# The last three down units of a decoder block, split 384 + 128 tokens in place of 256 + 256

## The chip, the cores and the metric

The kernel runs on one core of a Trainium2 chip. The metric is device time in microseconds (us). TensorE (PE, with its weight loads shown apart as PEld) multiplies into PSUM, VectorE (DVE) and ScalarE (ACT) read PSUM and work element by element, GpSimd (POOL) does a little early on, and SyncE (SP) issues all the loads and stores. A number in brackets after a kernel's time is the lowest and highest of its runs.

## The reference

One decoder block on a sequence of 512 tokens and 1024 channels: a mixer, then a squared-ReLU MLP, then a final RMSNorm. Only the end bears on this case:

```python
for i in range(DEPTH):                       # DEPTH = 1
    ...
    h = rmsnorm(x, norm_mlp_w[i]) * (1.0 + scale_f) + shift_f
    x = x + gate_f * (jnp.square(jax.nn.relu(h @ w_up[i])) @ w_down[i])
return rmsnorm(x, norm_final_w)
```

`w_down` is 4096 x 1024. The final norm needs, for each token, the mean square over all 1024 channels, so no token can be scaled before its last channel block is there.

## The kernel before, in words

Channels lie on the 128 partitions and tokens along the free dimension, so the 1024 channels of x are eight tiles of 128 x 512 (`x1[j]`, held in two large `xs` buffers). Each weight is loaded as float32 and split by `load_unit` into a high and a low float32r part (`hl` buffers, lines 131 and 132); activations are split in the same way (`s` buffers). A product is made of three matmuls, high times high, high times low, low times high (`mm3`, lines 141 to 143), and a "unit" is 8 blocks of 128 input channels, so 24 matmuls into one PSUM bank (`ps`). Every matmul loads its 128 x 128 weights anew.

The MLP goes over the 4096 hidden channels in four quarters. In the last quarter the output blocks j = 0 to 4 are made as whole units over 512 tokens. The last three, j = 5, 6, 7, are computed in two stretches of tokens: their weights are loaded once, then for each stretch the three units are multiplied over its tokens alone (72 matmuls), and after each unit come, on those tokens:

- `residual` (line 663 on DVE, 667 or 670 on ACT, 671 on DVE): x gets the gated unit added, its squares go into the running sum `ssum`, or for the last unit into `last_sq`; then line 754 on ACT scales x by the norm's weight.
- `norm` after the third unit: `column_sums` turns the squares into one sum for each token with matmuls of one moving column, one per 128 tokens and tile of squares (line 167 opens the sums, line 170 adds `ssum`, then `last_sq`); `rstd` makes square root (line 176, ACT) and reciprocal (line 177, DVE), puts them on the diagonal of one 128 x 128 block per 128 tokens (even blocks on DVE, line 183; odd ones on ACT, line 181), and spreads them over all partitions with one matmul that is as wide as the stretch (line 185).
- four multiplications on DVE (line 759), two channel tiles each over the stretch, and behind each a store on SP's queue (line 760).

The matmuls of lines 167, 170 and 185 have plain float32 operands, and each is executed as two weight loads and two matmul records. Those of lines 141 to 143 are one record each.

The order on each engine in this part is set by a scheduler at build time: it may place the norm's matmuls of the first stretch between the second stretch's unit matmuls. Each engine then works its list strictly in order. The `HALVES` of line 658 are (0, 256) and (256, 512).

## Time and profile before

| what | value |
|---|---|
| time, median of 3 runs | 998.27 us (997.61 to 998.98) |
| profiled execution: time | 997.95 us |
| profiled execution: span of its instructions | 996.2 us |
| mean granted TensorE clock | 0.992 |
| TensorE busy | 973.7 us, 98% of the span |
| VectorE busy | 623.8 us, 63% |
| ScalarE busy | 482.3 us, 48% |
| first unit matmul of the split part | 967.83 us |
| last unit matmul of the split part starts | 986.50 us |

Times within the profile count from the span's start. The profiled execution's own time is 1.75 us above its span, and it lies 0.32 us under the median. A busy share counts overlapping records as busy; what is worth reading in the end part is the distance between the starts of neighbouring instructions. In the groups a line of `rstd` or `column_sums` may belong to the first norm, the second or the last one.

### The profile page before, as it was taken

Reading aid. Unit: us, or ns where it says so; the run is one execution under the profiler, and the core shown is the slowest. Engines: PE = TensorE matmul, PEld = TensorE weight load, DVE = VectorE, ACT = ScalarE, POOL = GpSimd, SP = SyncE. Lnnn points to the kernel's source line nnn. Section 1 sums busy time; section 2 is a strip of 40 time slices with the busy share of each in tenths; the row PEclk is TensorE's granted clock in tenths of the full one; section 3 lists DMA queues with packets and bytes.
Section 4 is the critical chain, followed back from the end, with each engine's and each line's share of the span. In section 5 each row is a group of like instructions: output and inputs, shape, how many; then the busy total and the mean of one; then the engine's idle time right before and its main releaser. Section 6 shows DMA issues by size and latency. Waiting matters only on the chain.

```text
span 996.2 us, 12196 instructions
## 1 busy us (share of the span) xinstructions
PE 973.7 (98%) x4732; PEld 802.8 (81%) x4732; DVE 623.8 (63%) x887; ACT 482.3 (48%) x718; POOL 84.7 (9%) x79
## 2 busy tenths in 40 slices
PE   7899999999999999999999999999999999999996
PEld 6678777888778878788888888988888888888886
DVE  5978877586777776979775565654344334434443
ACT  5277999579648932553422343443133223313342
POOL 3510210211012012210000000000000000000000
PEclk8999999999999999999999999999999999999998
DMA  9725542442354233436886444032323232232302
GB/s 355 278 92 172 152 124 91 125 136 88 90 134 125 88 114 95 127 106 220 279 272 200 137 167 162 1 111 101 101 89 106 85 106 89 102 106 85 106 1 85
DMA packets 58620, 129.55 MB, mean 130 GB/s; under 512 B 4609, under 2 KB 29313, under 8 KB 58562
## 3 DMA queue, kind: packets, MB, share of 16 engines
q1 hardware_dynamic: 58562, 128.77, 40.1%
q8 instruction: 37, 0.61, 0.3%
q14 instruction: 21, 0.17, 0.1%
HBM read 126.53 MB, written 2.23 MB: 129 GB/s over the span
## 4 chain that ended last, share of the span: by engine, by line
PE 79%; ACT 8%; DVE 7%; DMA 2%; issue 2%; POOL 1%; SPq 1%; DVEq 0%; ACTq 0%; POOLq 0%
PE ps L141 25%; PE ps L142 24%; PE ps L143 24%; DMA mt<-cs_d 2%; ACT hl L131 1%; ACT L433 1%; DVE sz L157 1%; DVE xs L157 1%; PE ps L470 1%; PE ps L454 1%; ACT L350 1%; PE ps L447 1%; PE ps L281 1%; ACT L378 1%; DVE s L271 1%
## 5 line engine op out<-in xcount | busy, mean ns | idle before, releaser
L141 PE MATMUL ps<-s,hl 128*128 128x512 f32 (+1 forms) x1272 | 490.9, 386 | 1.3 <-ACT pad L529 1.2
L142 PE MATMUL ps<-s,hl 128*128 128x512 f32 (+1 forms) x1272 | 486.4, 382 | 0.0
L143 PE MATMUL ps<-s,hl 128*128 128x512 f32 (+1 forms) x1272 | 486.4, 383 | 0.0
L131 ACT CAST hl<-raw 128x1024 fp32r<-128x1024 f32 (+1 forms) x161 | 167.4, 1042 | 276.4 <-PE ps L142 269.0
L141 PEld LDWEIGHTS ps<-s,hl 128*128 128x128 f32 x1272 | 239.3, 188 | 50.4 <-issue 3.5
L142 PEld LDWEIGHTS ps<-s,hl 128*128 128x128 f32 x1272 | 239.4, 188 | 46.8 <-issue 1.4
L143 PEld LDWEIGHTS ps<-s,hl 128*128 128x128 f32 x1272 | 239.3, 188 | 46.8 <-issue 1.0
L132 DVE TENSOR_TENSOR hl<-raw,hl 128x1024 fp32r<-128x1024 f32 x153 | 189.9, 1243 | 126.5 <-ACT hl L131 123.5
L663 DVE SCALAR_TENSOR_TENSOR xs<-ps,mod,xs 128x512 f32<-128x512 f32 (+1 forms) x46 | 31.3, 680 | 106.8 <-PE ps L143 106.7
L111 ACT CAST s<-sz 128x512 fp32r<-128x512 f32 x52 | 31.5, 620 | 52.9 <-DVE sz L709 42.3
L157 DVE CUSTOM_DVE_ANT_0 raw<-raw,cbc,par_t 128x1024 f32<-128x1024 f32 x32 | 40.9, 1279 | 19.1 <-DMA raw<-adaT 19.0
L112 DVE TENSOR_TENSOR s<-sz,s 128x512 fp32r<-128x512 f32 x52 | 35.0, 689 | 22.8 <-ACT s L111 22.7
L433 ACT ACTIVATE mt<-mt,ncs 128x128 f32<-128x128 f32 x128 | 41.7, 392 | 13.2 <-POOL mt L429 12.9
L346 DVE SCALAR_TENSOR_TENSOR s<-ps,par_t,s 128x511 f32<-128x511 f32 (+2 forms) x54 | 40.2, 744 | 7.4 <-ACT s L344 6.9
L281 PE MATMUL ps<-s,hl 128*128 128x512 f32 x144 | 36.7, 410 | 5.8 <-ACT s L266 5.8
L281 PEld LDWEIGHTS ps<-s,hl 128*128 128x128 f32 x144 | 27.5, 196 | 14.3 <-ACT s L266 7.9
L429 POOL TENSOR_SCALAR_AFFINE_SELECT mt<-mt 128x1024 f32<-128x1024 f32 x16 | 19.5, 1224 | 215.4 <-ACT cd L426 99.0
L350 ACT ACT_TABLE_LOAD x19 | 24.4, 1283 | 7.0 <-DVE s L346 6.7
L433 ACT ACT_TABLE_LOAD x20 | 25.7, 1283 | 0.3
L492 ACT ACTIVATE s<-sz 128x512 f32<-128x512 f32 x16 | 10.1, 628 | 26.6 <-DVE sz L491 26.6
L111 ACT CAST s<-s 128x512 fp32r<-128x512 f32 x16 | 9.9, 622 | 25.5 <-DVE s L542 25.3
L709 DVE TENSOR_TENSOR sz<-sz 128x512 f32<-128x512 f32 x32 | 21.7, 684 | 0.0
(164 smaller groups left out, 783.7 us busy)
## 6 DMA issues: line engine op xcount, KB each, us to landing
raw<-adaT SPq DMA_DIRECT2D x32, 512.0 KB, 4.2
raw<-wup SPq DMA_DIRECT2D x32, 512.0 KB, 3.3
raw<-wdn SPq DMA_DIRECT2D x32, 512.0 KB, 3.3
raw<-wx SPq DMA_DIRECT2D x18, 512.0 KB, 3.5
raw<-wz SPq DMA_DIRECT2D x16, 512.0 KB, 4.0
mt<-cs_d SPq DMA_DIRECT2D x16, 512.0 KB, 5.9
raw<-wbs SPq DMA_DIRECT2D x16, 512.0 KB, 3.3
raw<-wgate SPq DMA_DIRECT2D x16, 512.0 KB, 3.7
```

The source lines that it names most:

```text
L111: act.copy(hi, src)
L112: dve.tensor_tensor(lo, src, hi.bitcast(F32), ALU.subtract)
L131: act.copy(hi[:, :w], r[:, a:a + w])
L132: (low or dve).tensor_tensor(lo[:, :w], r[:, a:a + w], hi[:, :w].bitcast(F32), ALU.subtract)
L141: pe.matmul(ps, whi, xhi[:, t0:t1], start=start, stop=False)
L142: pe.matmul(ps, whi, xlo[:, t0:t1], start=False, stop=False)
L143: pe.matmul(ps, wlo, xhi[:, t0:t1], start=False, stop=stop)
L157: dve.tensor_tensor_reduce(r, r, cbc, 1.0, col("b_ada", j), ALU.mult, ALU.add, mod[:, j:j + 1])
L281: pe.matmul(first[u], w[u][i // 2], h[k][i % 2], start=k == 0 and i == 0, stop=k == 7 and i == 2)
L346: dve.scalar_tensor_tensor(t[:, sh:], ps[:, :T - sh], w(3 - sh), t[:, sh:], ALU.mult, ALU.add)
L350: act.activation(o, t, AF.Silu)
L433: act.activation(m[:, i, :], m[:, i, :], AF.Exp, bias=ncs[:, c, g * HG + i:g * HG + i + 1])
```

## The change

The two stretches of the last three down units are now tokens 0 to 384 and 384 to 512. The split of the last three output-projection units (line 692) and of the first three up units (line 725) stays at halves.

```diff
         w = [load_unit(wdn[4 * j + 3]) for j in (5, 6, 7)]
         last_sq = F.get()
-        for t0, t1 in HALVES:
+        for t0, t1 in ((0, 3 * P), (3 * P, T)):
             for j in (5, 6, 7):
                 ps = PU.get()
                 for k in range(8):
```

No instruction is added to or taken from the total of any engine's list before the build's expansion; the shapes change, the one-column sums go from two and two to three and one, and the scheduler places some of them elsewhere.

On TensorE, early in the second stretch, between the second lot of column sums of the first norm (line 170, from the squares in `sz_826`) and the spreading matmul (line 185), the list before is:

```order
L170 MATMUL ps_1237_7548<-ones,sz_826_4732 128x1 x2
L141 MATMUL ps_1240_7569<-s_1179_7118,hl_1226_7446 128x256
L142 MATMUL ps_1240_7569<-s_1180_7119,hl_1226_7446 128x256
L143 MATMUL ps_1240_7569<-s_1179_7118,hl_1227_7447 128x256
L141 MATMUL ps_1240_7569<-s_1185_7155,hl_1226_7446 128x256
L142 MATMUL ps_1240_7569<-s_1186_7156,hl_1226_7446 128x256
L143 MATMUL ps_1240_7569<-s_1185_7155,hl_1227_7447 128x256
L141 MATMUL ps_1240_7569<-s_1191_7192,hl_1226_7446 128x256
L142 MATMUL ps_1240_7569<-s_1192_7193,hl_1226_7446 128x256
L143 MATMUL ps_1240_7569<-s_1191_7192,hl_1227_7447 128x256
L141 MATMUL ps_1240_7569<-s_1197_7229,hl_1226_7446 128x256
L185 MATMUL ps_1239_7559<-sz_825_4731,ones 128x256
```

and in the changed kernel:

```order
L170 MATMUL ps_1237_7548<-ones,sz_826_4732 128x1 x3
L141 MATMUL ps_1240_7572<-s_1173_7081,hl_1226_7446 128x128
L142 MATMUL ps_1240_7572<-s_1174_7082,hl_1226_7446 128x128
L143 MATMUL ps_1240_7572<-s_1173_7081,hl_1227_7447 128x128
L141 MATMUL ps_1240_7572<-s_1179_7118,hl_1226_7446 128x128
L142 MATMUL ps_1240_7572<-s_1180_7119,hl_1226_7446 128x128
L143 MATMUL ps_1240_7572<-s_1179_7118,hl_1227_7447 128x128
L185 MATMUL ps_1239_7562<-sz_825_4731,ones 128x384
```

So six unit matmuls of 128 tokens stand where ten of 256 stood, and the two norm steps around them are half again as large. Ahead of the first row shown, six unit matmuls follow the first lot of sums where nine did.

On DVE, from the first stretch's last residual to the second stretch's last one, the list before is:

```order
L663 SCALAR_TENSOR_TENSOR xs_824_4730<-ps_1236_7520,mod,xs_824_4730 128x256
L177 RECIPROCAL sm_1238_7554<-sm_1238_7554 128x2
L183 TENSOR_SCALAR sz_825_4731<-ident,sm_1238_7554 128x128
L759 TENSOR_TENSOR xs_823_4729<-xs_823_4729,ps_1239_7559 128x2x256 x2
L759 TENSOR_TENSOR xs_824_4730<-xs_824_4730,ps_1239_7559 128x2x256 x2
L663 SCALAR_TENSOR_TENSOR xs_824_4730<-ps_1240_7569,mod,xs_824_4730 128x256
L663 SCALAR_TENSOR_TENSOR xs_824_4730<-ps_1241_7598,mod,xs_824_4730 128x256
L671 TENSOR_TENSOR sz_825_4731<-sz_825_4731,sz_826_4732 128x256 x2
L663 SCALAR_TENSOR_TENSOR xs_824_4730<-ps_1242_7627,mod,xs_824_4730 128x256
```

and in the changed kernel:

```order
L663 SCALAR_TENSOR_TENSOR xs_824_4730<-ps_1236_7520,mod,xs_824_4730 128x384
L177 RECIPROCAL sm_1238_7556<-sm_1238_7556 128x3
L183 TENSOR_SCALAR sz_825_4731<-ident,sm_1238_7556 128x128 x2
L759 TENSOR_TENSOR xs_823_4729<-xs_823_4729,ps_1239_7562 128x2x384 x2
L759 TENSOR_TENSOR xs_824_4730<-xs_824_4730,ps_1239_7562 128x2x384 x2
L663 SCALAR_TENSOR_TENSOR xs_824_4730<-ps_1240_7572,mod,xs_824_4730 128x128
L671 TENSOR_TENSOR sz_825_4731<-sz_825_4731,sz_826_4732 128x128
L663 SCALAR_TENSOR_TENSOR xs_824_4730<-ps_1241_7601,mod,xs_824_4730 128x128
L671 TENSOR_TENSOR sz_825_4731<-sz_825_4731,sz_826_4732 128x128
L663 SCALAR_TENSOR_TENSOR xs_824_4730<-ps_1242_7630,mod,xs_824_4730 128x128
```

The diagonal of the first norm now has two blocks on DVE (tokens 0 to 128 and 256 to 384) and one on ACT; the second norm's only block is odd and lies on ACT alone. The four multiplications with the first norm have 768 elements per partition, those with the second 256; they were 512 and 512. The stores follow: four of 384 KB and four of 128 KB in place of eight of 256 KB, in the same places of SP's list.

## The prediction

> **What bounds the kernel now.** I read the page's chain that ended last first, by engine.

> ```profile
> PE 79%; ACT 8%; DVE 7%; DMA 2%; issue 2%; POOL 1%; SPq 1%; DVEq 0%; ACTq 0%; POOLq 0%
> ```

> TensorE is the bound almost everywhere, so the split part is read in two pieces: TensorE's stream to the last unit matmul, and the exposed tail behind it. The stream, from TensorE's timeline (start, length, instruction):

> ```profile
> 949.69 0.39 PE L142 MATMUL ps<-s,hl 128*128 128x512 f32 x1
> ...
> 967.60 0.39 PE L143 MATMUL ps<-s,hl 128*128 128x512 f32 x1
> 967.83 0.28 PE L141 MATMUL ps<-s,hl 128*128 128x256 f32 x1
> ...
> 976.34 0.28 PE L143 MATMUL ps<-s,hl 128*128 128x256 f32 x1
> 976.46 0.28 PE L167 MATMUL ps<-zeros,ones 128*128 128x2 f32 x2
> 976.60 0.59 PE L170 MATMUL ps<-ones,sz 128*128 128x1 f32 x4
> 977.04 0.37 PE L141 MATMUL ps<-s,hl 128*128 128x256 f32 x1
> ...
> 978.20 0.51 PE L170 MATMUL ps<-ones,sz 128*128 128x1 f32 x4
> 978.57 0.36 PE L141 MATMUL ps<-s,hl 128*128 128x256 f32 x1
> 978.77 0.28 PE L142 MATMUL ps<-s,hl 128*128 128x256 f32 x1
> ...
> 979.72 0.28 PE L141 MATMUL ps<-s,hl 128*128 128x256 f32 x1
> 979.84 0.59 PE L185 MATMUL ps<-sz,ones 128*128 128x256 f32 x2
> ...
> 980.50 0.28 PE L141 MATMUL ps<-s,hl 128*128 128x256 f32 x1
> ```

> Starts give the rate. 79 steps from 949.69 to 967.60 are 0.2267 us each at 512 tokens; 71 steps from 967.83 to 976.34 are 0.1199 at 256. The difference, 0.1068 per 256 tokens, is the price of streaming; 0.013 is fixed. No idle time stands in these rows, so TensorE never waits for the first norm now. The tail, from the chain of waits in order of time:

> ```profile
> 986.82 0.49 DVE xs L663
> 987.34 0.42 ACT sz L667
> 987.80 0.62 PE ps L170 x4
> 988.45 0.27 ACT sm L176
> 988.74 0.17 DVE sm L177
> 988.94 0.41 ACT sz L181
> 989.39 0.71 PE ps L185 x2
> 990.13 0.69 DVE xs L759
> ...
> 991.41 1.20 DVE xs L759 x2
> ```

> From 986.82 every engine works in turn on the second stretch alone, and behind the last multiplication come the stores, to 996.2: 9.4 us, of which all that scales with tokens can shrink.

> **The change part by part.** *First stretch, 72 matmuls of 384 tokens.* By the two rates each is 0.1199 + 0.0534 = 0.1733 us: 72 x 0.0534 = **+3.84**. If streaming were all, the second stretch would give this back.

> *Second stretch, 72 matmuls of 128 tokens.* No unit matmul as narrow as this is in the trace, so its pitch p is bounded. Streaming alone would give 0.1199 - 0.0534 = 0.067. But each matmul loads 128 weight columns, and these rows (groups, and one merged timeline row) show matmuls that stream less or no more and load as many:

> ```profile
> L170 PE MATMUL ps<-ones,sz 128*128 128x1 f32 x16 | 2.3, 247 | 0.5 <-ACT sz L667 0.5
> L447 PE MATMUL ps<-s,s 128*128 128x128 f32 x96 | 12.6, 275 | 0.0
> 103.94 1.05 PE L447 MATMUL ps<-s,s 128*128 128x128 f32 x8
> ```

> Line 170 streams one column and still needs (0.59 - 0.247) / 3 = 0.114 from record to record; line 447 needs (1.05 - 0.275) / 7 = 0.111. So with one column in place of 128 nothing is gained: the weight load sets a floor of 0.111 to 0.114 for plain float32, and float32r, whose loads pass in 0.1199 at 256 tokens, cannot have a higher floor than that. I take p = 0.116, the middle between 0.111 and 0.120: 72 x (0.116 - 0.1199) = **-0.28** (ends -0.64 and 0). The narrower half costs as much as before and the wider half costs more: this is the main term.

> [...]

> *Inserted norm matmuls.* Both lots of line 170 grow from 4 to 6 records: 4 x 0.114 = **+0.46**. Line 185: from L141 at 979.72 to L141 at 980.50 three steps take 0.78 in place of 0.36, so it costs 0.42, and half again as wide 0.63: **+0.21**.

> *A new wait at line 185.* Before, the diagonal was ready in time; the ScalarE and VectorE timelines:

> ```profile
> 978.74 0.26 ACT L176 ACTIVATE sm<-ps,eps_t 128x2 f32<-128x2 f32 x1 [0.61 <-PE ps L170]
> 979.24 0.40 ACT L181 ACTIVATE sz<-ident,sm 128x128 f32<-128x128 f32 x1 [0.23 <-DVE sm L177]
> 979.04 0.17 DVE L177 RECIPROCAL sm<-sm 128x2 f32<-128x2 f32 x1 [1.90 <-ACT sm L176]
> 979.24 0.29 DVE L183 TENSOR_SCALAR sz<-ident,sm 128x128 f32<-128x128 f32 x1
> ```

> It ended at 979.64, 0.20 before TensorE came to line 185. Counted from the start of the second lot of line 170, it will be ready after 0.54 + 0.23 (two records more) + 0.30 + 0.20 + 0.50 (two blocks on DVE, the second some 0.21 behind the first) + 0.05 = 1.82. TensorE, with six unit matmuls between, is there after 0.37 + 0.23 + 0.20 + 5p = 1.38. It stands still for **+0.44**, and 60 unit matmuls are queued behind it. The ends are 0 (if the diagonal's blocks run closer) and 0.5.

> The second lot of line 170 should just escape. TensorE reaches it 1.59 us behind line 167: it was 1.74 (976.46 to 978.20), two records more are +0.23, and five steps of 0.116 in place of eight of 0.120 are -0.38. Its squares come, with the slopes of the groups below, 0.38 + 0.61 + 0.04 + 0.53 = 1.56 behind the last wide matmul's start, and that lies 0.17 ahead of line 167: the margin is 0.20, less the 0.12 by which a weight load runs ahead.

> Together the last unit matmul is later by 3.84 - 0.28 + 0.46 + 0.21 + 0.44 = **+4.67**.

> *The tail at 128 tokens.* These groups of the last 30 us give the slopes of the element-wise steps:

> ```profile
> L663 DVE SCALAR_TENSOR_TENSOR xs<-ps,mod,xs 128x256 f32<-128x256 f32 x6 | 2.9, 482 | 5.8 <-PE ps L143 5.8
> L663 DVE SCALAR_TENSOR_TENSOR xs<-ps,mod,xs 128x512 f32<-128x512 f32 x1 | 0.7, 749 | 2.8 <-PE ps L143 2.8
> L670 ACT ACTIVATE sz<-xs 128x256 f32<-128x256 f32 x4 | 1.7, 418 | 7.0 <-DVE xs L663 6.9
> L670 ACT ACTIVATE sz<-xs 128x512 f32<-128x512 f32 x1 | 0.6, 631 | 4.0 <-DVE xs L663 4.0
> L671 DVE TENSOR_TENSOR sz<-sz 128x256 f32<-128x256 f32 x2 | 0.9, 426 | 1.0 <-ACT sz L670 1.0
> L759 DVE TENSOR_TENSOR xs<-xs,ps 128x512 f32<-128x512 f32 x8 | 5.0, 682 | 1.8 <-PE ps L185 1.8
> L760 SPq DMA_DIRECT2D out<-xs x8: 372/384/575, 981.2 to 992.7; - x8
> DMA to landing us min/median/max: 2.2/2.4/2.7
> 993.00:994.00 1.00, 0.00 (x0) 0.00 (x0) 0.00 (x0) 0.00 (x0) 0.00 (x0) 0.50 1.03 345
> ```

> 128 tokens fewer are -0.13 on line 663 (half of 749 - 482), -0.11 on the square, -0.05 on the last matmul, -0.23 for two records of line 170, -0.21 on line 185, -0.26 on the first multiplication (682 to about 426, the row of line 671): -0.99. Lines 176, 177 and 181 keep their length: one of two blocks is left, and it is the ACT one.

> The stores were issued 0.60 apart behind the multiplications. With these at a distance of 0.34 SP's own 0.384 a store sets the pace: 3 x (0.60 - 0.39) = -0.63. The last row (DMA share 1.03 at 345 GB/s) shows that the transfers themselves were packed; 128 KB less is up to 0.39 us, but each row of a store is then 512 bytes in place of 1024, so I take -0.2 (ends -0.4 and +0.3). The tail gives **-1.82**.

> **Sum:** +4.67 - 1.82 = **+2.85**. On the profiled execution's 997.95 that is 1000.8; that execution is 0.32 under the median, so against 998.27 it is **1001.1**. With all terms at their lower ends (p 0.111, no stall, stores -0.4) it is +1.85, so 1000.1; at their upper ends +3.7, so 1002.0.

> **The rivals.** *A, as above: weight loads set the narrow pitch.* For it speaks line 170, against it only that no narrow float32r matmul is seen.

> *C, not slower: the narrow matmuls stream at 0.067, and DVE becomes the bound.* The plain float32 floor need not hold for float32r. Then TensorE is early, and the four multiplications of 768 elements decide. Line 185 starts at about 983.56 (980.30 for the end of the wide stretch, 1.44 to the second lot, which now waits for its squares, 1.82 as above), the first multiplication 0.84 later (979.84 to 980.47 was 0.63, and 0.21 wider), and this row

> ```profile
> 980.47 2.48 DVE L759 TENSOR_TENSOR xs<-xs,ps 128x512 f32<-128x512 f32 x4 [0.94 <-PE ps L185]
> ```

> with 0.26 more for each gives 3.52: DVE is free at 987.92. Behind them in its list stand two rounds of residual, square and sum, about 1.0 each, so the last residual starts no earlier than 989.95, against 986.82 before: +3.13, less the tail's 1.77: +1.4, so 999.6, within 0.2%. It decides as soon as p is under 0.092.

> [...]

> *B, much slower: float32r narrower than 256 loses its single pass and goes at plain float32's rate.* In this kernel no float32r matmul is narrower than 256, and all that are 128 wide are plain, two records of 0.111 each. Then p = 0.222: 72 x (0.222 - 0.116) = +7.6, the wait at line 185 vanishes (-0.44), in all +10.0: 1008.3. Against it: the time has to come from the array itself, for the records at 512 and 256 show one fixed price and one slope.

> That the change moves other work is ruled out by the lists: nothing ahead of 967.83 differs, and the weights of all three units are there before it.

> **How the numbers follow.** A 0.68, B 0.13, C 0.13; 0.06 for what is not named, most of it a cheaper tail. Below 0.2%, 2.0 us here, a measurement of this kernel cannot tell a difference from none. A lies above 1000.3 but for a tenth: slower 0.61 + 0.13 + 0.01 = 0.75; same 0.07 of A, 0.12 of C, 0.02 of the rest, 0.21; faster 0.04. The range goes from C to somewhat beyond A's upper end, 999.0 to 1003.5; B is left out.

> **What would show it.** In the changed kernel's profile: unit matmuls of 384 at 0.173 from start to start, of 128 at 0.111 to 0.120 (A), 0.067 to 0.09 (C) or 0.22 (B); an idle time of about 0.4 us at line 185, released by DVE's line 183; the last unit matmul's start near 991.2; DVE with free time between line 759's four and the last residual; from the last residual to the span's end 7.6 us in place of 9.4. The prediction is wrong if p is outside 0.111 to 0.120, or if the stores do not come closer together.

## The result

| | before | changed |
|---|---|---|
| median | 999.55 us (997.61 to 1003.77, 19 runs) | 1005.07 us (999.73 to 1011.88, 19 runs) |
| profiled execution: time, span | 997.95, 996.2 us | 1007.3, 1005.6 us |
| mean granted clock of the profiled execution | 0.992 | 0.988 |
| first unit matmul of the split part to the last one's start | 18.67 us | 29.27 us |
| from there to the end of the span | 9.70 us | 8.42 us |

The change is slower by a ratio of 1.0059 (95% interval 1.0039 to 1.0079). Its runs are spread over 12 us: ten of the 19, with a mean granted clock of 0.992 or more, take 999.73 to 1005.07 us, and nine, with 0.982 to 0.988, take 1006.3 to 1011.88. The medians of the two groups are 1002.25 and 1008.70, and the median of all stands at the upper edge of the first group. The profiled execution is one of the nine.

TensorE's timeline of the changed kernel, at the same places as before (start, length, instruction, and in brackets the idle time ahead and what ended it):

```profile
980.42 0.28 PE L167 MATMUL ps<-zeros,ones 128*128 128x3 f32 x2
980.56 0.81 PE L170 MATMUL ps<-ones,sz 128*128 128x1 f32 x6
981.23 0.31 PE L141 MATMUL ps<-s,hl 128*128 128x128 f32 x1
...
981.82 0.28 PE L143 MATMUL ps<-s,hl 128*128 128x128 f32 x1
981.93 0.77 PE L170 MATMUL ps<-ones,sz 128*128 128x1 f32 x6
982.57 0.31 PE L141 MATMUL ps<-s,hl 128*128 128x128 f32 x1
982.71 0.28 PE L142 MATMUL ps<-s,hl 128*128 128x128 f32 x1
...
983.16 0.28 PE L143 MATMUL ps<-s,hl 128*128 128x128 f32 x1
983.88 1.02 PE L185 MATMUL ps<-sz,ones 128*128 128x384 f32 x2 [0.45 <-DVE sz L183]
...
985.02 0.41 PE L143 MATMUL ps<-s,hl 128*128 128x128 f32 x1
985.23 0.41 PE L141 MATMUL ps<-s,hl 128*128 128x128 f32 x1
...
997.18 0.41 PE L143 MATMUL ps<-s,hl 128*128 128x128 f32 x1
```

The wide stretch runs from 967.91 to 980.42, 3.88 us longer than before. The first twelve narrow matmuls come at the forecast pitch: 982.71 to 983.16 are four steps of 0.112. Behind line 185 the same instruction takes 0.2133 from start to start (985.02 to 997.18, 57 steps), nearly twice as long. The table by stretches gives the reason in its eighth column, the granted clock (the first column is the stretch, then its length, busy time and instructions of PE, PEld, DVE, ACT, POOL; after the clock, DMA share and GB/s):

```profile
977.67:981.08 3.41, 3.41 (x24) 3.41 (x22) 1.01 (x2) 0.61 (x1) 0.00 (x0) 1.00 0.00 0
981.08:984.50 3.42, 2.97 (x24) 2.70 (x23) 0.82 (x4) 1.80 (x4) 0.00 (x0) 1.00 0.00 0
984.50:987.91 3.41, 3.41 (x17) 3.21 (x16) 2.97 (x4) 0.00 (x0) 0.00 (x0) 0.50 0.33 114
991.32:994.74 3.42, 3.42 (x18) 3.42 (x18) 0.64 (x2) 0.71 (x2) 0.00 (x0) 0.50 0.00 0
```

The clock falls to half at 984.50 and stays there to the end: 18 instructions pass in 3.4 us where 33 pass at full clock (the first experiment below). TensorE's steps in the tail, from the chain of waits, run at half clock too:

```profile
997.60 0.33 PE ps L167 x2
997.92 0.43 PE ps L170 x2
998.38 0.60 PE ps L170 x2
999.00 0.27 ACT sm L176
999.50 0.41 ACT sz L181
999.95 0.81 PE ps L185 x2
1000.78 0.42 DVE xs L759
...
1001.54 0.66 DVE xs L759 x2
```

Line 170's two records take 0.60 where four took 0.62 before, and line 185 takes 0.81 where 0.71 stood, although each has half the tokens. The element-wise steps did shrink as forecast (the first multiplication 0.69 to 0.42), and so the tail is 1.28 us shorter and not 1.82.

The stores did come closer together, 0.47, 0.52 and 0.53 from issue to issue where 0.59, 0.64 and 0.59 stood before, but not to the forecast 0.39.

So two questions are open: what halves the clock, and what the change would cost without it.

### The profile page after: what moved, and what is told of

It is laid out like the page before. It is cut to its first block, busy times and chain, and to the rows that moved or that the text cites. A ratio compares the mean times of both kernels' runs of the same rounds, so it can differ in the third digit from the quotient of the medians.

```text
span 1005.6 us, 12194 instructions
## 1 busy us (share of the span) xinstructions
PE 985.4 (98%) x4732; PEld 812.5 (81%) x4732; DVE 624.1 (62%) x887; ACT 482.7 (48%) x718; POOL 84.7 (8%) x79
## 4 chain that ended last, share of the span: by engine, by line
PE 78%; ACT 8%; DVE 7%; DMA 3%; issue 2%; POOL 1%; SPq 1%; DVEq 0%; ACTq 0%; POOLq 0%
PE ps L141 24%; PE ps L142 24%; PE ps L143 24%; DMA mt<-cs_d 3%; ACT hl L131 1%; DVE xs L157 1%; DVE sz L157 1%; ACT L433 1%; PE ps L470 1%; PE ps L454 1%; ACT L350 1%; PE ps L447 1%; PE ps L281 1%; DVE s L271 1%; ACT L378 1%
## 5 line engine op out<-in xcount | busy, mean ns | idle before, releaser
L141 PE MATMUL ps<-s,hl 128*128 128x512 f32 (+3 forms) x1272 | 494.4, 389 | 1.3 <-ACT pad L529 1.2
L143 PE MATMUL ps<-s,hl 128*128 128x512 f32 (+3 forms) x1272 | 489.7, 385 | 0.0
L142 PE MATMUL ps<-s,hl 128*128 128x512 f32 (+3 forms) x1272 | 489.6, 385 | 0.0
L141 PEld LDWEIGHTS ps<-s,hl 128*128 128x128 f32 x1272 | 241.7, 190 | 50.5 <-issue 3.5
L142 PEld LDWEIGHTS ps<-s,hl 128*128 128x128 f32 x1272 | 242.0, 190 | 47.1 <-issue 1.7
L143 PEld LDWEIGHTS ps<-s,hl 128*128 128x128 f32 x1272 | 241.9, 190 | 47.2 <-issue 1.0
L663 DVE SCALAR_TENSOR_TENSOR xs<-ps,mod,xs 128x512 f32<-128x512 f32 (+3 forms) x46 | 31.3, 681 | 114.8 <-PE ps L143 114.6
L670 ACT ACTIVATE sz<-xs 128x512 f32<-128x512 f32 (+3 forms) x18 | 9.2, 513 | 27.8 <-DVE xs L663 26.2
```

Of the source, the lines that this page charges most:

```text
L141: pe.matmul(ps, whi, xhi[:, t0:t1], start=start, stop=False)
L142: pe.matmul(ps, whi, xlo[:, t0:t1], start=False, stop=False)
L143: pe.matmul(ps, wlo, xhi[:, t0:t1], start=False, stop=stop)
```

## The experiments

"Clock gate", or "gate", stands here for whatever grants TensorE its clock, which is 1.00 or 0.50 in these traces. In them the clock changes on borders that lie whole multiples of 3.41 us apart: in the kernel before it is 0.50 from 11.37 to 18.20, from 28.44 to 31.85 and from 991.00 on, in the change from 15.11 to 18.52 and from 984.50 on. The stretch between two borders is called a window. The ratios below compare with the kernel before on the same chip: 1000.11 us (23 runs) for the first four experiments, 999.58 (18 runs) for the others but the repetitions. Two theories at first. **G**: narrow matmuls alone are too sparse (0.053 us of streaming in each 0.111) and make the clock gate take the array for idle. **W**: the narrow matmuls pass, and the idle time at line 185 with the one-column sums around it brings the clock down.

**The narrow stretch first.**

```diff
-        for t0, t1 in ((0, 3 * P), (3 * P, T)):
+        for t0, t1 in ((0, P), (P, T)):
```

> The stretches in the other order, tokens 0 to 128 and then 128 to 512, so the 72 narrow matmuls stand directly behind dense ones, with no wait ahead of them. Theory G (the clock gate takes a 3.4 us window full of 128-wide matmuls for idle, because the array streams only some 0.053 of each 0.111 us): the granted clock falls to 0.5 within 3.4 to 7 us of the first narrow matmul, the pitch goes from 0.111 to 0.213, and the clock comes back 3 to 7 us into the 384-wide matmuls. Theory W (the idle time at line 185 together with the one-column sums brings the clock down, and the narrow matmuls by themselves do not): the clock stays 1.00 and the pitch 0.111 up to the sums of the first norm at least. The exposed tail is 384 tokens wide here, some 4 us longer than before, so both expect a time above 1003; G 2 to 5 us more than W, 1006 to 1010.

Measured: 1004.56 us (1003.33 to 1008.57, 10 runs), ratio 1.0046 (1.0032 to 1.0061). Two whole windows of nothing but narrow matmuls, by stretches:

```profile
970.36:973.77 3.41, 3.41 (x33) 3.41 (x33) 1.34 (x3) 1.88 (x4) 0.00 (x0) 1.00 0.00 0
973.77:977.18 3.41, 3.41 (x33) 3.41 (x32) 0.64 (x2) 0.71 (x2) 0.00 (x0) 1.00 0.00 0
```

33 records in each and the clock at 1.00 there, in the window before and in the windows behind until the tail (994.25). G is wrong in this form: narrow matmuls alone do not bring the clock down.

**The norm's matmuls later, so that nothing waits.**

```diff
+        units(0, 3 * P, (5, 6, 7))
+        units(3 * P, T, (5,))
+        rd = diagonal(0, 3 * P)
+        units(3 * P, T, (6,))
+        finish(0, 3 * P, *rd)
+        units(3 * P, T, (7,))
+        finish(3 * P, T, *diagonal(3 * P, T))
```

These are the last lines of the edit. The three functions defined above them hold the change's own code in three parts: `units` is the unit matmuls with their residuals, `diagonal` the sums, square root, reciprocal and diagonal blocks, `finish` the spreading matmul, the multiplications and the stores.

> The split 384 + 128 of the change, but the sums of the first norm are placed behind the second stretch's first unit (24 narrow matmuls) and line 185's matmul behind its second unit, so that TensorE waits for neither. G: the clock still falls to 0.5 in the second stretch, pitch 0.213, a median of 1003 to 1008 and a spread of several us like the change's. W: the clock stays 1.00 to the tail, pitch 0.111, 1000 to 1002, with a spread like the kernel before.

Measured: 1006.46 us (1004.31 to 1010.37, 6 runs), ratio 1.0064 (1.0041 to 1.0087). TensorE has no idle time in the second stretch, and yet:

```profile
983.60:987.02 3.42, 3.42 (x33) 3.42 (x32) 0.97 (x2) 1.14 (x2) 0.00 (x0) 1.00 0.00 0
987.02:990.43 3.41, 3.41 (x33) 3.41 (x32) 0.86 (x4) 1.16 (x4) 0.00 (x0) 1.00 0.02 5
990.43:993.84 3.41, 3.41 (x15) 2.80 (x14) 1.94 (x4) 0.71 (x2) 0.00 (x0) 0.50 0.00 0
```

So the wait is not needed either, and the 1000 to 1002 us that W expected did not come. The window that ends in half clock holds seven of the twelve one-column records of line 170 (they start at 986.49) and narrow matmuls; the one before it, with the other five, does not.

**The narrow stretch with 256 columns streamed.**

```diff
-                    mm3(ps[:, t0:t1], w[j - 5][k], us[k], k == 0, k == 7, t0, t1)
+                    s0 = min(t0, 2 * P)
+                    mm3(ps[:, s0:t1], w[j - 5][k], us[k], k == 0, k == 7, s0, t1)
```

> The split 384 + 128 of the change in everything but the unit matmuls of the second stretch, which stream tokens 256 to 512 again (the 128 tokens in front are computed a second time and not read). Each takes 0.120 and streams 0.107 of it, as in the kernel before. G: the clock stays 1.00 up to the tail; the last unit matmul is later than before by 3.84 + 0.46 + 0.21, the tail shorter by 1.8, so 2.7 us over before, 1001.0, and the spread is that of before. If the clock falls here as well, the sparse streaming is not its cause: 1004 or more.

Measured: 1001.52 us (999.79 to 1005.80, 12 runs), ratio 1.0016 (1.0003 to 1.0030); the clock falls only in the tail, at 995.7. The split part, from its first unit matmul to the span's end, takes 31.01 us, 2.64 more than before: the forecast 2.7. By the medians the difference is 1.41 us, and the interval hardly excludes none. The window with the sums and the one behind it:

```profile
982.05:985.47 3.42, 3.42 (x30) 3.42 (x30) 0.73 (x4) 1.81 (x4) 0.00 (x0) 1.00 0.00 0
985.47:988.88 3.41, 3.41 (x27) 3.14 (x26) 2.54 (x3) 0.00 (x0) 0.00 (x0) 1.00 0.19 68
```

This is the change without the lost clock, and it is still no faster than the kernel before.

**The narrow matmuls as plain float32.**

```diff
-                    mm3(ps[:, t0:t1], w[j - 5][k], us[k], k == 0, k == 7, t0, t1)
+                    f = (lambda p: tuple(v.bitcast(F32) for v in p)) if t0 else (lambda p: p)
+                    mm3(ps[:, t0:t1], f(w[j - 5][k]), f(us[k]), k == 0, k == 7, t0, t1)
```

> The change, with the 72 narrow matmuls read as plain float32 (same values), each then two records of 0.111 that stream nearly all the time. G (the share of time in which the array streams counts): the clock stays 1.00 in the second stretch, 0.222 for each matmul, so 3.84 + 7.3 + 0.7 - 1.8 = 10 us over before, 1008, with a small spread. If it is the narrow width or the share of weight loads that counts, the clock falls here too and a matmul takes up to 0.43: 1012 to 1022.

Measured: 1009.26 us (1008.98 to 1009.40, 4 runs), ratio 1.0086 (1.0063 to 1.0109). From TensorE's timeline:

```profile
998.49 0.39 PE L142 MATMUL ps<-s,hl 128*128 128x128 f32 x2
998.71 0.39 PE L143 MATMUL ps<-s,hl 128*128 128x128 f32 x2
```

0.222 a matmul, the clock at 1.00 until 1005.1, and four runs within 0.4 us. Plain float32 streams twice as long for each record (in seven of the twelve pairs in the kernel before, line 454's two records of 512 columns are 0.43 us apart from start to start, in the others 0.50 to 0.54; line 141's are 0.2267) and each matmul is two records; the number and the width of the weight loads are what they were or more. So in this run the clock goes with the streaming and not with the width.

These four runs leave a theory **T**: the gate looks at how much was streamed in each window of 3.4 us. Narrow matmuls alone stream enough to keep the clock. One-column sums stream next to nothing, and a window shared by them and narrow matmuls can fall short.

**The sums 128 columns wide.**

```diff
-            R = norm(t0, t1, [ssum, last_sq])
...
+            pe.matmul(ps[:, t0:t1], ones, nil[:, t0:t1], start=True, stop=False)
+            for i, sq in enumerate([ssum, last_sq]):
+                for c in range(c0, c1):
+                    pe.matmul(ps[:, c * P:(c + 1) * P], sq[:, c * P:(c + 1) * P], ones, start=False,
...
```

In the lines left out, `nil` is set to zero and `rstd` reads one column in 128 of the sums.

> The change, but each sum of squares of the last two norms (line 170) streams 128 columns of ones in place of one. Its weight load takes 0.111 as before, so it takes TensorE no longer; the array just streams meanwhile. The opening matmul has 384 columns and costs 0.4 us more. Line 185 now stands behind five unit matmuls, so its wait is no shorter than the change's 0.7 us between starts. Theory T (the gate counts what was streamed in each 3.4 us window; narrow matmuls alone, 48% of the time, pass, as in the run with the narrow stretch first; one-column sums and wait in the same window press the count under the bound, and at half clock the narrow matmuls, 25%, cannot lift it again): the clock stays 1.00 to the tail, pitch 0.111, median 1.5 to 3 us over before. Theory W (the wait itself brings the clock down): it falls to 0.5 at the next window border as in the change, median 5 us or more over before.

Measured: 1002.97 us (1002.79 to 1004.73, 6 runs), ratio 1.0039 (1.0024 to 1.0054). The sums (line 762 here), the wait and the narrow matmuls behind it, then the stretches:

```profile
982.31 1.72 PE L762 MATMUL ps<-ones,sz 128*128 128x128 f32 x12
985.20 0.88 PE L185 MATMUL ps<-sz,ones 128*128 128x384 f32 x2 [0.66 <-DVE sz L183]
...
985.98 0.28 PE L141 MATMUL ps<-s,hl 128*128 128x128 f32 x1
...
993.24 0.27 PE L143 MATMUL ps<-s,hl 128*128 128x128 f32 x1
```

```profile
982.73:986.15 3.42, 2.76 (x20) 2.23 (x19) 0.69 (x4) 1.59 (x4) 0.00 (x0) 1.00 0.00 0
986.15:989.56 3.41, 3.41 (x33) 3.41 (x32) 3.41 (x4) 0.00 (x0) 0.00 (x0) 1.00 0.34 117
```

The window holds a longer wait than the change's (0.66 against 0.45) and fewer instructions, 20 against 24, yet the clock stays 1.00, and 65 narrow steps take 0.1117 each. So the wait by itself does not bring the clock down, and T held. By the medians the runs are 3.4 us over before, above the expected 1.5 to 3; the wide opening matmul and the longer wait are some 0.85 of it (from the first unit matmul of the split part to the last takes 24.08 us here, 23.23 in the third repetition below).

**Both norms behind the last unit.**

```diff
+        for t0, t1 in ((0, 3 * P), (3 * P, T)):
             R = norm(t0, t1, [ssum, last_sq])
```

> The change with both norms behind the last unit, so that the 72 narrow matmuls stand in one piece with no sum and no wait among them. T: the clock stays 1.00 through all 72, pitch 0.111, and falls only in the tail, in every run. G (a window of narrow matmuls alone is taken for idle): it falls within 3.4 to 7 us of their start in at least some of the runs. The last unit matmul comes at 3.84 - 0.6 - 1.5 = 1.7 us later than before; the tail is longer by two norms' sums and 512 tokens' multiplications and stores, some 4 us: 5 to 7 over before by T, 8 to 14 by G.

Measured: 1004.52 us (1004.18 to 1006.10, 4 runs), ratio 1.0054 (1.0036 to 1.0073). All 72 narrow matmuls pass at full clock:

```profile
983.16:986.58 3.42, 3.42 (x33) 3.42 (x33) 0.99 (x3) 0.99 (x3) 0.00 (x0) 1.00 0.02 5
986.58:989.99 3.41, 3.41 (x33) 3.41 (x32) 0.64 (x2) 0.44 (x2) 0.00 (x0) 1.00 0.00 0
989.99:993.40 3.41, 3.30 (x11) 2.35 (x10) 1.32 (x5) 1.81 (x6) 0.00 (x0) 0.50 0.00 0
```

The clock falls only at 989.99, behind the sums from 988.40 on, and the time is 4.9 us over before, just under the 5 to 7 that T expected.

**192 columns streamed.**

```diff
-                    s0 = min(t0, 2 * P)
+                    s0 = min(t0, 320)
```

> The change with 192 columns streamed by each unit matmul of the second stretch (tokens 320 to 512, the first 64 not read). The weight load still sets 0.111 a matmul at full clock and 0.213 at half; 72% of the time is streamed at full clock. Only four unit matmuls stand between the sums' lots and four ahead of line 185, so sums, wait and few matmuls fall together as in the change, or more so. T with a bound just under 48%: the clock falls in some runs, as in the change, and at half clock the matmuls stream 0.37 of the full rate, which tells whether that lifts it again. If the matmuls' own density decides alone: clock 1.00, 1 to 2.5 us over before.

Measured: 1004.45 us (1002.29 to 1007.69, 5 runs), ratio 1.0056 (1.0036 to 1.0076):

```profile
979.95:983.36 3.41, 3.38 (x27) 3.08 (x25) 0.81 (x3) 1.42 (x4) 0.00 (x0) 1.00 0.00 0
983.36:986.78 3.42, 2.81 (x9) 2.24 (x10) 1.62 (x4) 0.38 (x1) 0.00 (x0) 0.50 0.00 0
986.78:990.19 3.41, 3.41 (x18) 3.41 (x17) 2.94 (x5) 0.70 (x2) 0.00 (x0) 0.50 0.63 220
990.19:993.60 3.41, 3.41 (x33) 3.41 (x33) 0.64 (x2) 0.73 (x3) 0.00 (x0) 1.00 0.68 246
```

Between the lots of sums stand only four unit matmuls here, and the clock falls as in the change. But after two windows it comes back, among the same unit matmuls. At half clock 128 columns never lifted it (984.50 to the end in the change), 192 did.

**The change again, three times.** The borders of the windows lie elsewhere in each execution. The second and the third have one comment line more.

> The changed kernel itself once more. The borders of the 3.4 us windows lie elsewhere in each execution. T: where a border parts the two lots of one-column sums and the wait at line 185, neither window is sparse enough, the clock stays 1.00 to the tail, the narrow pitch is 0.111 throughout and the time is that of the sum, 2.5 to 3 us over before; where one window holds both lots and the wait, the clock falls at its end and stays at 0.5 until the last unit matmul, 6 to 11 us over before. G (narrow matmuls alone) and W (the wait) would bring it down in every execution.

> The changed kernel once more, for another position of the windows: as for the first repetition.

> The changed kernel once more, for a third position of the windows: as for the first repetition.

Measured, each one run beside one run of before at 1002.81: 1009.35, 1005.00 and 1001.54 us. In the first the clock falls at 985.16, with all twelve sums and most of the wait in one window. In the other two it stays 1.00 to the tail. By G, and by W in either form, it would have fallen in all three. The third, from TensorE's timeline and by stretches:

```profile
981.20 0.81 PE L170 MATMUL ps<-ones,sz 128*128 128x1 f32 x6
982.57 0.78 PE L170 MATMUL ps<-ones,sz 128*128 128x1 f32 x6
984.52 0.88 PE L185 MATMUL ps<-sz,ones 128*128 128x384 f32 x2 [0.45 <-DVE sz L183]
991.78 0.28 PE L143 MATMUL ps<-s,hl 128*128 128x128 f32 x1
```

```profile
979.46:982.87 3.41, 3.41 (x28) 3.41 (x27) 0.62 (x1) 0.93 (x2) 0.00 (x0) 1.00 0.00 0
982.87:986.28 3.41, 2.96 (x23) 2.58 (x23) 1.50 (x4) 0.88 (x3) 0.00 (x0) 1.00 0.02 5
```

Here a border at 982.87 falls into the second lot of sums, so that the first lot and the wait lie in different windows, and the clock stays, though the instructions are the same to the last one. This is the change at its own price: 31.25 us from the first unit matmul of the split part (968.55) to the end of the span, against 28.37 before: +2.88. The second repetition gives 31.52, +3.15 (its 1005.00 holds other losses, one of them a window of half clock at 354 us); the first gives 38.23, +9.86, and the profiled execution above 37.69, +9.32. These are stretches of the trace against the profiled execution of before; as times of single runs the third repetition is 1.27 us under the run of before beside it. The two groups of the 19 runs say the same as the stretches: their medians are 2.70 and 9.15 over before's 999.55.

**How sparse is too sparse.** I worked out for whole windows which share of the time the array streamed, from starts and widths in the timelines: 0.417 ns a column for float32r (0.1068 us per 256), twice that for each of the two records of plain float32, and double at half clock (in the kernel before, line 281's float32r records of 512 columns are 0.427 us apart at half clock, from 28.76 to 31.75, where line 141's are 0.2267 at full clock). The share is good to some 0.02, since a border can fall within a matmul.

| kernel, window | streamed share | clock in the window, then |
|---|---|---|
| first repetition, 981.75 to 985.16 | 0.22 | 1.00, then 0.50 |
| the change, 981.08 to 984.50 | 0.35 | 1.00, then 0.50 |
| 192 columns, 979.95 to 983.36 | 0.35 | 1.00, then 0.50 |
| norm later, 987.02 to 990.43 | 0.36 | 1.00, then 0.50 |
| plain float32, 998.27 to 1001.68 | 0.38 | 1.00, then 1.00 |
| norm later, 983.60 to 987.02 | 0.39 | 1.00, then 1.00 |
| second repetition, 985.86 to 989.28 | 0.41 | 1.00, then 1.00 |
| third repetition, 982.87 to 986.28 | 0.44 | 1.00, then 1.00 |
| narrow stretch first, 973.77 to 977.18 | 0.47 | 1.00, then 1.00 |
| wide sums, 982.73 to 986.15 | 0.57 | 1.00, then 1.00 |
| 256 columns, 982.05 to 985.47 | 0.68 | 1.00, then 1.00 |
| the change, 987.91 to 991.32 | 0.50 | 0.50, then 0.50 |
| 192 columns, 983.36 to 986.78 | 0.70 | 0.50, then 0.50 |
| 192 columns, 986.78 to 990.19 | 0.75 | 0.50, then 1.00 |

One order without an exception in the table: at 0.36 and under the next window is at half clock, at 0.38 and over it is not; at half clock 0.70 did not lift it and 0.75 did. The rest of the thirteen traces agrees (line 470's matmuls, which start in pairs, are counted once a pair), with one window on the wrong side by less than the reckoning's error: in the kernel before, 25.02 to 28.44 streamed 0.39 and the clock fell. The half-clock window at 354 us of the second repetition fits too: 0.37 was streamed ahead of it, where TensorE stood idle for 2.09 us.

The half-clock rows can be read in a second way. At half clock a column takes twice as long, so in columns streamed they are worth half: 0.25, 0.35 and 0.375 of what the full clock could stream in a window. Then one bound, near 0.37, fits the falls and the rise alike. The runs do not tell two bounds in time from one bound in columns. That the quantity is exactly the streaming is an inference from these windows; another measure that ranks them in the same way would fit as well.

**Another split of the kernel before: only its last two units in halves.**

```diff
-            for j in range(8 if q < 3 else 5):
+            for j in range(8 if q < 3 else 6):
...
-            for j in (5, 6, 7):
+            for j in (6, 7):
...
```

> From the kernel before: only the last two units in halves, 256 + 256, the unit j = 5 whole. 24 matmuls of 512 in place of 48 of 256: 24 x (0.2267 - 0.2398) = -0.3 us, and the rest as before, since the first norm still ends under the second stretch's 48 matmuls (5.8 us). Both theories: clock 1.00 to the tail, 0.1 to 0.5 us under before, within 0.2%.

Measured: 1000.14 us (998.67 to 1006.05, 12 runs), ratio 1.0013 (0.9998 to 1.0027): no gain where 0.1 to 0.5 us was expected. The saving of 0.3 in the stream is lost in the tail, which takes 10.57 us from the last unit matmul's start in place of 9.70: both lots of sums now stand together behind the units and wait for a sum on DVE (0.79), and the clock falls at 990.0, before line 185. No version that was run beats the kernel before.

## Why the prediction was wrong

The sign was right and the size was not: 1001.1 was forecast, 999.0 to 1003.5 as range, and the median is 1005.07. The step that failed is the second term of the sum, "72 matmuls of 128 tokens", where one pitch p was taken for all of them. Its size was right at full clock, but the granted clock was not part of the step, nor of any rival. In the profiled execution twelve had 0.112 and 60 had 0.2133: about +5.5 in place of -0.28. The tail lost some 0.6 to the same half clock: 8.42 us, against 7.79 in the run with 256 columns streamed, whose norm in the tail runs at full clock. A smaller part of the miss is the base: the forecast stood on 998.27, the median of three runs of before, and over 19 runs it is 999.55. The difference itself is 5.52 us where 2.85 was forecast.

Point by point:

- *The wide stretch*, +3.84: 12.51 us for 72 matmuls in the profiled execution and in the third repetition alike, +3.88. Right.
- *The weight-load floor*, 0.111 to 0.120: 0.1117 with float32r at full clock. The lower end was right; 0.116 was a little too high. Rival C's 0.067 is seen in no run.
- *The inserted norm matmuls and the new wait*: the wait is 0.45 (forecast 0.44), released by DVE's line 183. From line 167 to the last unit matmul's start the third repetition takes 10.72 us against 10.04 before, +0.68, where -0.28 + 0.46 + 0.21 + 0.44 = 0.83 was forecast. The lower pitch alone is worth -0.31, so the inserted steps and the wait cost some 0.16 more than forecast.
- *The tail*, -1.82: 8.02 us against 9.70 in that repetition, -1.68, although its line 185 already ran at half clock (0.81 in the chain, where 0.50 was expected). With the full clock, in the run with 256 columns streamed, it is -1.91. That the sum comes so near is in part luck: the stores are 0.46 to 0.53 apart in the third repetition where 0.39 was forecast. The -0.2 for stores of 128 KB was an estimate; in the profiled execution each of them landed 1.9 us after its issue, where the last four of 256 KB before took 2.2 to 2.5.
- *The sum*, +2.85: +2.88 in the third repetition, +3.15 in the second, +2.70 between the medians of the ten runs and of before. At full clock the sum was right.
- *Rival B* (float32r under 256 columns at plain float32's rate, 1008.3) forecast a time like those of the runs with the lower clock, and 0.2133 looks like its 0.222. It is wrong all the same: its mechanism would hold for all 72 matmuls, and in the run with the norms last all 72 pass at full clock and in the profiled execution the first twelve at 0.112.
- *The signs that I named*: the wait and DVE's free time were where they were expected, and so was the pitch in the third repetition; in the profiled execution the pitch of 60 matmuls lay outside 0.111 to 0.120, which was the sign of being wrong. The last unit matmul near 991.2 came at 991.78 in the third repetition (which began 0.72 later) and at 997.18 in the profiled execution. What should have stood among them is the granted clock behind the sums.

What the profile before could have told: the row from 993 to 994 that the prediction quotes for its DMA share has the clock at 0.50, behind the sparse steps of the tail. I took that stretch for an idle TensorE and did not ask what the same steps would do amid matmuls that stream half of the time. Before, the window with the first lot of sums still streamed 0.72 to 0.79 by the same reckoning, so there was room. With matmuls at 0.48 there is little: the sparsest window ahead of the tail streamed 0.22, 0.35, 0.41 and 0.44 in the four executions of the change.

## What to carry to other kernels

A matmul of 256 float32r columns took 0.1199 us here, one of 192 or 128 took 0.1117 at full clock, and line 170's records of a single column were 0.114 apart: under 256 columns nearly all of the price stays, which fits a weight load that has to pass in any case. So splitting tokens more unevenly moved cost into the wide part (+3.88) without a like saving in the narrow one. And look at what the array streams, not only at gaps: sparse matmuls, tiny reductions among them and a wait of 0.45 us cost the clock together in two of the four traced executions of the change, and in the profiled one, where the matmuls stayed narrow, it did not come back. Streaming 192 columns under the same weight load took no longer here than 128, and it helped: 192 columns brought the clock back, and 256 columns, or sums 128 columns wide, kept it.
